# Heads turned four tiles behind their sums, attention in three pinned steps, weight sums on DVE

## The chip, the cores and the metric

The kernel runs as one program on one core of a Trainium2 chip. The core's engines work from queues of their own, each in the order in which its program stands: TensorE (PE) multiplies, VectorE (DVE), ScalarE (ACT) and GpSimd (POOL) do the elementwise work, SyncE (SP) only issues transfers. An instruction that waits for another engine holds up all that stands behind it on its own. The metric is the device time of one execution in microseconds (us), lower is better.

## The reference, cut to what matters

```python
def reference(x, mem, ...):                       # x (1, 1024, 1024) float32
    for l in range(DEPTH):                        # layer 0: attention, layer 1: HGRN2
        h = rms_norm(x, norm_gain[l])
        cols = h @ w_in                           # mixer columns | memory query | gate
        mix = dilated_mixer(...) if l % 2 == 0 else hgrn2_mixer(...)
        mem_out = memory_cross_attention(q_mem, mem, ...)
        y = concatenate([mix, mem_out]) * silu(gate)
        x = x + y @ w_out
    return x

def dilated_mixer(cols, cos, sin, q_gain, k_gain):
    qkv = cols.reshape(B, S, 3, N_GROUPS, A_HEADS, HEAD_DIM)     # 3 groups of 8 heads of 128
    q, k = rms_norm(q, q_gain), rms_norm(k, k_gain)              # over each head's 128 columns
    q, k = apply_partial_rotary(q, ...), apply_partial_rotary(k, ...)
    # causal windows (128, 1), (512, 4), (2048, 16); the groups merged by their denominators
```

## The kernel before

All products are made in float32 accuracy from halves: an operand is split into a high part (`hi`, `wh`) and a low rest (`lo`, `wl`), and three matmuls of 512 columns take the place of one. ACT makes the high part (`copy`, L154), DVE the rest (L838, L200).

The program runs in stages. First come the norm of `x`, its transposes, sums of its blocks and a chunk of the gate (to about 74 us). Then, to 853 us, come the **products**: the q, k and v columns of attention's three groups, nine blocks in the order k, v, q for groups 2, 1, 0. Each block is worked as seven products of quarter blocks in the manner of Strassen and Winograd (`product`, p = 0 to 6), each of four tiles (i = 0 to 3) of 12 matmuls, L932 to L934, into a PSUM bank `acc` of pool `pp`, which has three. The quarter weights arrive as `raw` by SP's queue; their sums and differences are made by `combine` (L842, eight for a block, on POOL), then they are split (`split_side`).

A product's tile is added to kept sums `x0` to `x3`, `y0` to `y3`. In products 1, 4, 5 and 6 this finishes 128 rows by 512 columns, four heads, of the block, held in a tile `c` (three buffers) or in `x`, `y`. For q and k a **chain** follows (`projected`, L893): DVE adds the bank (L942, L953, L957 or L960); ACT squares (L899); DVE reduces (L901) and scales (L161, `rv`); POOL takes the power (L163, `rr`); DVE multiplies (L903); POOL turns the rotary columns with four instructions (L876, L878 twice, L880); PE transposes four times (`heads_T`, L298) into a bank `pt`, of which there are two; ACT moves that into a tile `os` (L910); ACT's queue then spills it to memory, `qk_scr`: four transfers of 64 KB for groups 2 and 1 (L918), one of 256 KB for group 0 (L913). For v the sum is only spilled. So 16 chains run in each of six blocks, in bursts: four in product 1, then twelve in products 4 to 6.

The order of instructions on every engine is chosen when the program is built, by a scheduler that plans with costs of its own; the written order binds it only through data and buffers. On the chip that order is fixed.

Next is the **memory stage** (853 to 1032 us): slices of 48 matmuls of layer 0's gate for the memory output (`gate_mem`: the two of `MG0`, and the first of `MG1`, which is written at the start of attention and which the scheduler moved in here), the norm of `mem`, its products and the memory queries. Then **attention** (1032 to 1262 us): 12 pairs of heads, group 2 first, then 1, then 0, eight tiles each. `fetch` brings a pair's k, q and v (1024 KB each) into one of two buffers; per tile `scores` makes the scores (L1078), DVE's masked minimum (L1081) and ACT's exponentials (L1083), and `values` transposes them (L1093), copies that to `pts` (L1095, DVE) and multiplies by v (L1101). Every second tile of groups 2 and 1, `spill` copies the bank to one of two tiles `os` (ACT, L154) and sends it to memory (L1121, `o_scr`); in group 0 `merge` reads those again. The second slice of `MG1` stands after group 1. The rest, gate, output product and layer 1, runs to the end.

Of the kernel before, what the change touches and what calls it, by code (L numbers as in the profile page):

```python
# [30 lines left out]
D = 1024  # L31
# [71 lines left out]
def trunk_kernel(ctx, tc, x, mem, pos, norm_gain, w_in_a, q_gain_a, k_gain_a, qk_gain_t, w_out_a,  # L103
# [6 lines left out]
    const = ctx.enter_context(tc.tile_pool(name="const", bufs=1))  # L110
    hpool = ctx.enter_context(tc.tile_pool(name="hT", bufs=1))
    wpool = ctx.enter_context(tc.tile_pool(name="wring", bufs=WR))
    rpool = ctx.enter_context(tc.tile_pool(name="raw", bufs=2))
    gs = ctx.enter_context(tc.tile_pool(name="gs", bufs=2))
    small = ctx.enter_context(tc.tile_pool(name="small", bufs=6))

    small.tile([128, 40], F32, name="left", bufs=1)
    ctx.enter_context(tc.tile_pool(name="right", bufs=1, side="right")).tile([128, 56], F32, name="right")
    dram = ctx.enter_context(tc.tile_pool(name="scratch", bufs=1, space=bass.MemoryType.DRAM))
    pp = ctx.enter_context(tc.tile_pool(name="pp", bufs=3, space=PSUM))  # L120
    pS = ctx.enter_context(tc.tile_pool(name="pS", bufs=2, space=PSUM))
    pT = ctx.enter_context(tc.tile_pool(name="pT", bufs=2, space=PSUM))
    pO = ctx.enter_context(tc.tile_pool(name="pO", bufs=1, space=PSUM))
# [20 lines left out]
    V.memset(nhalf[:], -0.5)  # L144

# [24 lines left out]
    def more_weights(stack, n=2, start=0):  # L170

        more.append(stack.enter_context(tc.tile_pool(name="wmore", bufs=n, side="right")))
        more.append(WR + n)
        turn[0] = start
        stack.callback(more.clear)
# [129 lines left out]
    def mem_gains(pool):  # L305

        rows_ = pool.tile([16, 128], F32, name="mgr", bufs=1)
# [5 lines left out]
    def mem_norm(pool):  # L313

        mts = []
        for m in range(2):
            xt = pool.tile([128, D], F32, name="xt")
            Y.dma_start(xt[:], mem[m * 128:(m + 1) * 128, :])
            xn = norm_rows(xt[:], None, D, pool)
# [146 lines left out]
    def feature_proj(key):  # L466
# [3 lines left out]
        for hf in range(2):  # L470
# [7 lines left out]
            pss.append(ps)  # L478
        return pss

    def gate_slice(key, scr, pool=gs, name="os", gain=None):


        for hf, ps in enumerate(feature_proj(key)):
# [11 lines left out]
    def gate_mem(i, *where):  # L496
        gate_slice(("gate_m", i), gatem_scr[i * 128:(i + 1) * 128], *where)
# [136 lines left out]
    def begin_out_a(s2):  # L634
        assert at_piece[1] == at_piece[0] and not rooms
        more_weights(wide, W_B, WR)
        early, late = (s2.enter_context(tc.tile_pool(name=n, bufs=3, side="right")) for n in ("wearly", "wlate"))
# [3 lines left out]
        ol, oy, op = (s2.enter_context(tc.tile_pool(name=n, bufs=1)) for n in ("outl", "outy", "outp"))  # L641
# [55 lines left out]
    with ExitStack() as sa:  # L697
        atab = sa.enter_context(tc.tile_pool(name="atab", bufs=1))
# [6 lines left out]
        ext = sx.enter_context(tc.tile_pool(name="ext", bufs=1))  # L705
        sums = {(s, n): ext.tile([128, 4, 512], F32R, name=s + n) for s in ("s2", "s3", "s4") for n in ("hi", "lo")}
        wx = sx.enter_context(tc.tile_pool(name="wx", bufs=1))
# [11 lines left out]
        def tables():  # L719
# [35 lines left out]
            V.memset(gqk[0:ROT, :], 1.0)  # L755

        s0 = ExitStack()
        ipool = s0.enter_context(tc.tile_pool(name="ipool", bufs=1))
# [82 lines left out]
        def combine(gi, out, a, b, h):  # L841
            G.tensor_tensor(raws[gi, out, h], raws[gi, a, h], raws[gi, b, h], op=OP.subtract)  # L842
# [50 lines left out]
        def projected(i, g, Q, m, c):  # L893
# [14 lines left out]
            to = o[:] if g == 0 else o[:].rearrange("p h (r l) -> p h l r", r=n)  # L908
            of = t[:] if g == 0 else t[:].rearrange("p h (l r) -> p h l r", r=n)
            A.activation(to, of, AF.Copy, scale=gqk[:, g:g + 1] if i else 1.0)  # L910
            scr = qk_scr[i][g][:, 4 * Q:4 * Q + 4]
            if g == 0:
                SQ.dma_start(scr[:, :, m * 128:(m + 1) * 128], o[:])  # L913
                return
            at = m % 4 * 32 if g == 1 else m * 16
            view = scr.rearrange("p h (a r c) -> p h a r c", a=3 - g, r=n)[:, :, m // 4 if g == 1 else 0, :, at:at + RUN[g]]
            for h in range(4):
                SQ.dma_start(view[:, h], o[:, h].rearrange("p (r l) -> p r l", r=n))  # L918
# [608 lines left out]
```

## Time and profile before

| what | value |
|---|---|
| time, median of 3 runs | 2194.97 us (2194.24 to 2196.37) |
| the profiled execution | 2194.4 us, its span 2192.5 us |
| mean granted PE clock | 0.988 |
| DMA | 272.53 MB, mean 124 GB/s |
| products, 74 to 853 us | 779 us, PE busy 748.5 |
| memory stage, 853 to 1032 us | 179 us, PE busy 169.5 |
| attention, 1032 to 1262 us | 230 us, PE busy 191.2 |

A row that groups instructions names line, engine, operation and tiles; after the x its count, then the busy time, the mean in ns, and behind the bar the engine's idle time just before them and what ended it. A row of the waits reads: engine, tile and line that waited, the engine, tile and line that ended it, the sum in us, how often, the longest.

### The profile page before, as it was taken

What the parts mean: (1) busy time and instruction counts of PE and PEld (TensorE: products, weight loads), DVE (VectorE), ACT (ScalarE), POOL (GpSimd) and SP (SyncE); (2) the same over time, 40 slices, a digit from 0 to 9 for tenths busy, and PEclk for the clock granted to TensorE, in tenths of its full rate; (3) what the DMA queues carried; (4) which work ended last, traced back from release to release, by engine and by line L of the source; (5) the groups of instructions that cost most, each with busy time, mean ns of one, the idle gap of its engine ahead of it and who ended that gap; (6) DMA issues with size and microseconds to landing.
All of it is one profiled execution on the core that took longest, in us unless ns stands there. A gap on an engine that the chain in (4) does not pass through costs nothing.

```text
span 2192.5 us, 29737 instructions
## 1 busy us (share of the span) xinstructions
PE 2093.1 (95%) x10713; PEld 1744.3 (80%) x10713; DVE 1300.3 (59%) x2524; ACT 827.6 (38%) x1567; POOL 745.5 (34%) x772
## 2 busy tenths in 40 slices
PE   7999998999999999897889899999999999999999
PEld 5777876778777888686778788888888888888887
DVE  7875566745767455645556954433557772776443
ACT  5544345443444233545554322233533222232211
POOL 2777278763888366022002610011300000000221
PEclk9999999999999999999899999999999999999999
DMA  5366365452544524523886666431211112113733
GB/s 185 116 122 110 106 120 94 100 125 93 130 95 121 151 76 125 158 74 128 317 285 220 205 216 205 144 109 39 87 39 49 58 58 58 49 50 96 231 119 112
DMA packets 416322, 272.53 MB, mean 124 GB/s; under 512 B 223392, under 2 KB 347568, under 8 KB 413104
## 3 DMA queue, kind: packets, MB, share of 16 engines
q1 hardware_dynamic: 152608, 189.72, 28.2%
q10 hardware_dynamic: 263568, 80.91, 14.5%
q8 instruction: 86, 1.41, 0.3%
q14 instruction: 60, 0.49, 0.1%
HBM read 187.60 MB, written 82.97 MB: 123 GB/s over the span
## 4 chain that ended last, share of the span: by engine, by line
PE 44%; DMA 3%; DVE 2%; ACT 1%; issue 0%; ACTq 0%; POOL 0%; SPq 0%; DVEq 0%
PE acc L475 5%; PE acc L474 5%; PE acc L476 5%; PE acc L562 4%; PE acc L563 4%; PE acc L564 4%; PE acc L240 3%; PE acc L238 3%; PE acc L239 3%; DMA o_scr<-os 2%; PE pt L1282 1%; PE s L1282 1%; PE s L1078 1%; PE po L1416 1%; PE pt L281 1%; PE s L1385 1%
## 5 line engine op out<-in xcount | busy, mean ns | idle before, releaser
L163 POOL TENSOR_TENSOR rr<-rv,nhalf 128x4 f32<-128x4 f32 (+1 forms) x150 | 162.4, 1088 | 782.3 <-DVE rv L161 765.4
L154 ACT ACTIVATE wh<-raw 128x1024 fp32r<-128x1024 f32 x206 | 215.6, 1056 | 256.6 <-PE acc L934 123.6
L838 DVE TENSOR_TENSOR wl<-raw,wh 128x1024 fp32r<-128x1024 f32 x126 | 189.3, 1509 | 109.0 <-ACT wh L154 108.7
L932 PE MATMUL acc<-wh,hhi 128*128 128x512 f32 x576 | 229.4, 398 | 11.8 <-ACT x L154 11.2
L842 POOL TENSOR_TENSOR raw<-raw 128x1024 f32<-128x1024 f32 x72 | 176.5, 2470 | 170.3 <-DVE wl L838 133.9
L933 PE MATMUL acc<-wl,hhi 128*128 128x512 f32 x576 | 227.7, 395 | 0.0
L934 PE MATMUL acc<-wh,hlo 128*128 128x512 f32 x576 | 227.5, 395 | 0.0
L475 PE MATMUL acc<-hlo,wh 128*128 128x512 f32 x512 | 204.1, 399 | 0.0
L476 PE MATMUL acc<-hhi,wl 128*128 128x512 f32 x512 | 203.9, 398 | 0.0
L474 PE MATMUL acc<-hhi,wh 128*128 128x512 f32 x512 | 202.9, 396 | 0.0
L200 DVE TENSOR_TENSOR wl<-raw,wh 128x1024 fp32r<-128x1024 f32 x80 | 98.5, 1234 | 121.2 <-ACT wh L154 120.6
L240 PE MATMUL acc<-wh,hlo 128*128 128x512 f32 x384 | 151.6, 396 | 5.8 <-DVE hlo L259 5.8
L238 PE MATMUL acc<-wh,hhi 128*128 128x512 f32 x384 | 150.8, 397 | 0.8 <-ACT wh L154 0.8
L239 PE MATMUL acc<-wl,hhi 128*128 128x512 f32 x384 | 151.3, 394 | 0.0
L562 PE MATMUL acc<-wh,yhi 128*128 128x512 f32 x360 | 144.4, 403 | 0.5 <-ACT yhi L154 0.5
L563 PE MATMUL acc<-wl,yhi 128*128 128x512 f32 x360 | 142.8, 397 | 0.0
L564 PE MATMUL acc<-wh,ylo 128*128 128x512 f32 x360 | 141.5, 398 | 0.0
L932 PEld LDWEIGHTS acc<-wh,hhi 128*128 128x128 f32 x576 | 109.4, 190 | 37.2 <-ACT x L154 13.7
L934 PEld LDWEIGHTS acc<-wh,hlo 128*128 128x128 f32 x576 | 109.3, 190 | 22.4
L933 PEld LDWEIGHTS acc<-wl,hhi 128*128 128x128 f32 x576 | 109.4, 190 | 22.1 <-DVE wl L838 0.3
L474 PEld LDWEIGHTS acc<-hhi,wh 128*128 128x128 f32 x512 | 96.3, 188 | 17.9
L475 PEld LDWEIGHTS acc<-hlo,wh 128*128 128x128 f32 x512 | 96.3, 188 | 17.9
(287 smaller groups left out, 4799.1 us busy)
## 6 DMA issues: line engine op xcount, KB each, us to landing
raw<-in_w_in_a_dram SPq DMA_DIRECT2D x106, 512.0 KB, 4.2
raw<-in_w_in_b_dram SPq DMA_DIRECT2D x40, 512.0 KB, 3.7
qk_scr<-os ACTq DMA_DIRECT2D x256, 64.0 KB, 2.7
kT<-qk_scr SPq DMA_DIRECT2D x12, 1024.0 KB, 5.8
qT<-qk_scr SPq DMA_DIRECT2D x12, 1024.0 KB, 8.7
o_scr<-os ACTq DMA_DIRECT2D x96, 128.0 KB, 4.0
qk_scr<-os ACTq DMA_DIRECT2D x32, 256.0 KB, 2.2
raw<-in_w_mem_kv_dram SPq DMA_DIRECT2D x16, 512.0 KB, 3.7
```

The costliest lines, as they stand in the source:

```text
L238: T.matmul(ps, hi, wh[:, j, :], start=at == 0, stop=False)
L239: T.matmul(ps, hi, wl[:, j, :], start=False, stop=False)
L240: T.matmul(ps, lo, wh[:, j, :], start=False, stop=at == n - 1)
L474: T.matmul(ps[:], wh[:, k, :], mh, start=k == 0, stop=False)
L475: T.matmul(ps[:], wh[:, k, :], ml, start=False, stop=False)
L476: T.matmul(ps[:], wl[:, k, :], mh, start=False, stop=k == 7)
L562: T.matmul(pss[ch][:], hi[:, k, :], wh[:, j, :], start=first and k == 0, stop=False)
L563: T.matmul(pss[ch][:], hi[:, k, :], wl[:, j, :], start=False, stop=False)
L564: T.matmul(pss[ch][:], lo[:, k, :], wh[:, j, :], start=False, stop=end and k == 3)
L932: T.matmul(flat, hi, wh, start=kt == 0, stop=False)
L933: T.matmul(flat, hi, wl, start=False, stop=False)
L934: T.matmul(flat, lo, wh, start=False, stop=kt == 3)
```

## The change

- **Pools**: all take `reuse_waits="tile"`: whoever takes freed space waits for the tiles that lay there, not for their whole pool.
- **Order**: in products and attention PE's instructions are tied to the order in which they are written (`pinned`).
- **Chains**: the transposes, ACT's copy and the spill of a finished tile are a function of their own, `spill_heads`, which `passed` calls when the fourth tile in the count has passed (the third for the last tile of product 1). They are written in place into the tile that held the sum; the fourth tile of products 1 and 4 gets a room of its own (`y3`, `os`). In every second product the fourth tile goes to bank `po`. Groups 2 and 1 spill by one transfer of 256 KB.
- **Weight sums**: six of a block's eight `combine` go from POOL to DVE; those named 21' stay.
- **Memory stage**: the memory's norm is written ahead of the first gate slice, its transposes behind; the gain table is made at the start.
- **Attention**: the first pair is fetched before the memory queries into a pool of its own, and two pools take turns. A step does the scores of tile j, the transposes of tile j-1, one matmul of the gate slices (96 in 96 steps, in place of the slice that the scheduler had moved into the memory stage and the one after group 1), and the values of tile j-2. In group 0 ACT makes the copy `pts`.

```diff
-    const = ctx.enter_context(tc.tile_pool(name="const", bufs=1))
+    const = ctx.enter_context(tc.tile_pool(name="const", bufs=1, reuse_waits="tile"))
...
+    @contextmanager
+    def pinned():
+
+        traced = nc.cur_bb.bb.instructions
+        n = len(traced)
+        yield
+        mine = lambda i: i.engine == mybir.EngineType.PE
+        last = next((i for i in reversed(traced[:n]) if mine(i)), None)
+        for i in traced[n:]:
+            if mine(i):
+                if last is not None:
+                    tc.add_manual_dep(i, last.name, mybir.DependencyInfo(mybir.DependencyClass.NoSync, mybir.DependencyReason.DATA),
+                                      reason="pinned")
+                last = i
...
+    def gate_mem_steps(i):
+
+        (wh, wl), = take(("gate_m", i), 1)
+        for hf in range(2):
+            ps = pp.tile([128, 512], F32, name="acc")
+            for k in range(8):
+                mh, ml = (hT(n, k)[:, hf * 512:(hf + 1) * 512] for n in ("hi", "lo"))
+                for j, (w, m) in enumerate(((wh, mh), (wh, ml), (wl, mh))):
+                    T.matmul(ps[:], w[:, k, :], m, start=k == 0 and j == 0, stop=k == 7 and j == 2)
+                    yield
...
         def combine(gi, out, a, b, h):
-            G.tensor_tensor(raws[gi, out, h], raws[gi, a, h], raws[gi, b, h], op=OP.subtract)
+            (G if out == "21'" else V).tensor_tensor(raws[gi, out, h], raws[gi, a, h], raws[gi, b, h], op=OP.subtract)
...
-        def projected(i, g, Q, m, c):
+        tick, due = [0], []
+
+        def passed(n=1):
+
+            tick[0] += n
+            while due and due[0][0] <= tick[0]:
+                due.pop(0)[1]()
+
+        def projected(i, g, Q, m, c, after):
...
             rotary(c, m)
+            due.append((tick[0] + after, lambda: spill_heads(i, g, Q, m, c)))
+
+        def spill_heads(i, g, Q, m, c):
+
             t = heads_T(c)
-            o = gs.tile([128, 4, 128], F32, name="os")
+            o = c
...
-            view = scr.rearrange("p h (a r c) -> p h a r c", a=3 - g, r=n)[:, :, m // 4 if g == 1 else 0, :, at:at + RUN[g]]
-            for h in range(4):
-                SQ.dma_start(view[:, h], o[:, h].rearrange("p (r l) -> p r l", r=n))
+            flat = qk_scr[i][g].rearrange("p h s -> p (h s)")
+            o0, w, at = (m // 4 * 4096 + Q * 2048, 2048, m % 4 * 32) if g == 1 else (Q * 4096, 4096, m * 16)
+            SQ.dma_start(flat[:, o0:o0 + w].rearrange("p (x c) -> p x c", c=128)[:, :, at:at + RUN[g]],
+                         o.rearrange("p h (r l) -> p (h r) l", r=n))
...
-                ps = pp.tile([128, 4, 128], F32, name="acc")[:]
+                bank, name = (pO, "po") if n % 2 == 0 and i == 3 else (pp, "acc")
+                ps = bank.tile([128, 4, 128], F32, name=name)[:]
...
-                    c = room("c", bufs=3)
+                    c = room("c", bufs=3) if i < 3 else room("y3")
                     V.tensor_tensor(c, xs[i], ps, op=OP.add)
                     copy(A, xs[i], ps)
-                    projected(i_, g, 0, i, c)
+                    projected(i_, g, 0, i, c, 4 if i < 3 else 3)
...
                 weights_ahead(n, i)
+                passed()
...
-            product(n, (lambda i, h: ahead(1 + h) if i == 3 else None) if n == last else None)
+            with pinned():
+                product(n, (lambda i, h: ahead(3 + h) if i == 3 else ahead(2)) if n == last else None)
...
-                mem_gains(ipool)
-                gate_mem(MG0[0])
-                mts = mem_norm(ipool)
+                xns = mem_norm(ipool)
+                gate_mem(MG0[0], between=lambda: passed(2))
+                passed(2)
+                mts = mem_turn(ipool, xns)
                 gate_mem(MG0[1])
...
+            fetch(0)
             mem_queries("qmem_a", km, vm, *mp, lambda: mp[1].tile([128, 2, MEM], F32, name="pm")[:], om_scr, lhs_natural)
...
-                V.tensor_copy(pts[:, :2 * nb, :], t[:, :2 * nb, :])
+                copy(V if g else A, pts[:, :2 * nb, :], t[:, :2 * nb, :])
+                return g, hp, m, pts, blocks
...
-            gate_mem(MG1[0])
             fetch(1)
...
                 for m in range(NT):
-                    new = (g, hp, m, *scores(g, hp, m))
-                    if waiting:
-                        values(*waiting.pop())
-                    waiting.append(new)
-                if (g, hp) == (1, 3):
-                    gate_mem(MG1[1])
+                    with pinned():
+                        new = (g, hp, m, *scores(g, hp, m))
+                        old = turn_(*scored.pop()) if scored else None
+                        next(fill, None)
+                        if turned:
+                            values(*turned.pop())
+                    scored.append(new)
+                    if old:
+                        turned.append(old)
```

Three places in the instruction order, all in the block of k for group 1 (the fourth of nine), at the end of product 1. First PE: before, the transposes of the first tile of product 1, `c_3228`, stand here (`acc_3463` is the first tile of product 3):

```order
L933 MATMUL acc_3463<-wl_3413,s2hi_131 128x512
L934 MATMUL acc_3463<-wh_3412,s2lo_132 128x512
L298 MATMUL pt_3246<-ident_119,c_3228 128x128 x4
L298 MATMUL pt_3296<-ident_119,c_3278 128x128 x4
L932 MATMUL acc_3490<-wh_3408,s2hi_131 128x512
L933 MATMUL acc_3490<-wl_3409,s2hi_131 128x512
```

And with the change, where that tile is `c_3105` and `po_3195` is the fourth tile of product 1 itself:

```order
L983 MATMUL po_3195<-wh_3014,hhi_143 128x512
L984 MATMUL po_3195<-wl_3015,hhi_143 128x512
L985 MATMUL po_3195<-wh_3014,hlo_144 128x512
L313 MATMUL pt_3226<-ident_119,c_3105 128x128 x4
L983 MATMUL acc_3233<-wh_3123,hhi_143 128x512
L984 MATMUL acc_3233<-wl_3124,hhi_143 128x512
```

The transposes stood behind the eighth tile after the one that they turn; they now stand behind the third, the last of the burst.

On DVE, before, the first three tiles of product 1 get their multiplication (L903) in a row, and the fourth's add (`c_3364`, L942) comes later, behind two adds of product 3 (L949):

```order
L903 TENSOR_TENSOR c_3228<-c_3228,rr4_3237 128x512
L903 TENSOR_TENSOR c_3278<-c_3278,rr4_3287 128x512
L903 TENSOR_TENSOR c_3321<-c_3321,rr4_3330 128x512
L838 TENSOR_TENSOR wl_3479<-raw_2565,wh_3478 128x1024
L838 TENSOR_TENSOR wl_3483<-raw_2664,wh_3482 128x1024
L949 TENSOR_TENSOR x0_3152<-x0_3152,acc_3463 128x512
L942 TENSOR_TENSOR c_3364<-x3_3213,acc_3351 128x512
```

With the change (L881 weight sum, L993 add, L948 reduce, L176 scale, L877 low half, L950 multiply):

```order
L881 TENSOR_TENSOR raw_2582<-raw_3020,raw_2582 128x1024
L993 TENSOR_TENSOR c_3144<-x1_3044,acc_3131 128x512
L881 TENSOR_TENSOR raw_2578<-raw_2582,raw_2578 128x1024
L948 TENSOR_REDUCE ss4_3110<-s_3108 128x4
L993 TENSOR_TENSOR c_3176<-x2_3067,acc_3163 128x512
L948 TENSOR_REDUCE ss4_3149<-s_3147 128x4
L176 TENSOR_SCALAR rv4_3112<-ss4_3110 128x4
L176 TENSOR_SCALAR rv4_3151<-ss4_3149 128x4
L877 TENSOR_TENSOR wl_3249<-raw_2580,wh_3248 128x1024
L993 TENSOR_TENSOR y3_3208<-x3_3090,po_3195 128x512
L950 TENSOR_TENSOR c_3105<-c_3105,rr4_3114 128x512
L948 TENSOR_REDUCE ss4_3181<-s_3179 128x4
```

The multiplication of the first tile, `c_3105`, now stands right behind the add of the fourth, which needs `po_3195`, the last matmuls ahead of the transposes above. Two weight sums stand between the adds shown.

On POOL, before, six weight sums (L842, three of them shown) lie around the powers (L163), and the rotary of the first tile (`c_3228`) follows:

```order
L842 TENSOR_TENSOR raw_3166<-raw_2666,raw_3166 128x1024
L842 TENSOR_TENSOR raw_2664<-raw_2668,raw_2664 128x1024
L163 TENSOR_TENSOR rr4_3237<-rv4_3235,nhalf_118 128x4
L163 TENSOR_TENSOR rr4_3287<-rv4_3285,nhalf_118 128x4
L163 TENSOR_TENSOR rr4_3330<-rv4_3328,nhalf_118 128x4
L842 TENSOR_TENSOR raw_3486<-raw_2668,raw_3486 128x1024
L876 TENSOR_TENSOR t1_3240<-c_3228,rc_688 128x128
L878 TENSOR_TENSOR t2_3241<-c_3228,rs_689 128x4x16 x2
L880 TENSOR_TENSOR c_3228<-t1_3240,t2_3241 128x4x32
```

With the change (L881 weight sum, L178 power, L915 to L919 rotary):

```order
L915 TENSOR_TENSOR t1_3117<-c_3105,rc_693 128x128
L917 TENSOR_TENSOR t2_3118<-c_3105,rs_694 128x4x16 x2
L919 TENSOR_TENSOR c_3105<-t1_3117,t2_3118 128x4x32
L881 TENSOR_TENSOR raw_3347<-raw_2582,raw_3347 128x1024
L915 TENSOR_TENSOR t1_3156<-c_3144,rc_693 128x128
L917 TENSOR_TENSOR t2_3157<-c_3144,rs_694 128x4x16 x2
L178 TENSOR_TENSOR rr4_3185<-rv4_3183,nhalf_118 128x4
L178 TENSOR_TENSOR rr4_3217<-rv4_3215,nhalf_118 128x4
L919 TENSOR_TENSOR c_3144<-t1_3156,t2_3157 128x4x32
```

One weight sum of POOL is now between the rotary of the first tile and that of the second, `c_3144`, and two powers stand inside the latter. These three orders are alike in all six blocks of k and q.

More of the change, by code (lines that the diff above doesn't have):

```diff
@@ L1 @@
 import math
-from contextlib import ExitStack
+from contextlib import ExitStack, contextmanager
 import numpy as np
@@ L170, in more_weights @@
     def more_weights(stack, n=2, start=0):
-        more.append(stack.enter_context(tc.tile_pool(name="wmore", bufs=n, side="right")))
+        more.append(stack.enter_context(tc.tile_pool(name="wmore", bufs=n, side="right", reuse_waits="tile")))
         more.append(WR + n)
@@ L478, in feature_proj, with gate_slice @@
             pss.append(ps)
-        return pss
-    def gate_slice(key, scr, pool=gs, name="os", gain=None):
-        for hf, ps in enumerate(feature_proj(key)):
+            if between and hf == 0:
+                between()
+        return pss
+    def gate_slice(key, scr, pool=gs, name="os", gain=None, between=None):
+        for hf, ps in enumerate(feature_proj(key, between)):
             sg = pool.tile([128, 4, 128], F32, name=name)[:].rearrange("p h d -> p (h d)")
@@ L1085, in scores, with turn_ @@
                 return p, blocks
-            def values(g, hp, m, p, blocks):
-                q, k, v, st = held[g, hp]
+            def turn_(g, hp, m, p, blocks):
                 nb = len(blocks)
```

192 lines of the change are left out of this document (111 added, 81 removed).

## The prediction

> **What bounds the kernel now.** The page first, then PE stage by stage, then what ended its waits.
>
> ```profile
> span 2192.5 us, 29737 instructions
> PE 2093.1 (95%) x10713; PEld 1744.3 (80%) x10713; DVE 1300.3 (59%) x2524; ACT 827.6 (38%) x1567; POOL 745.5 (34%) x772
> ```
>
> PE bounds the whole, so time can be won or lost only where it idles or runs at a lower clock. In the table by stages the first number behind the comma is PE's busy time; PEclk is the granted clock.
>
> ```profile
> core 0: us, PE busy (x) PEld busy (x) DVE busy (x) ACT busy (x) POOL busy (x), PEclk, DMA share, GB/s
> 74.00:853.00 779.00, 748.50 (x3386) 605.32 (x3384) 503.29 (x644) 325.23 (x421) 535.98 (x572) 0.99 0.47 112
> 853.00:1032.00 179.00, 169.52 (x872) 140.62 (x871) 94.94 (x178) 85.17 (x177) 41.28 (x50) 0.97 0.37 111
> 1032.00:1262.00 230.00, 191.20 (x1283) 170.59 (x1283) 141.35 (x601) 113.27 (x437) 46.37 (x41) 0.94 0.78 259
> 1262.00:2192.00 930.00, 925.59 (x4923) 782.56 (x4921) 502.49 (x1003) 258.11 (x455) 95.49 (x86) 1.00 0.32 101
> ```
>
> PE idles for 30.5 us in the products, 9.5 in the memory stage, 38.8 in attention, and 4.4 in the last 930, where nothing is to be had. In the products a clock of 0.99 costs about 0.01 x 748.5 = 7.5 us more, so some 741 us are work at full clock. PE's waits, in the products and then in attention:
>
> ```profile
> PE pt L298 <- POOL c L880: 13.2, 13, 2.5
> PE acc L932 <- ACT x L154: 11.2, 6, 2.9
> ...
> PE po L1101 <- ACT os L154: 12.6, 6, 5.1
> PE s L1078 <- DMA qT<-qk_scr: 9.6, 2, 9.2
> ```
>
> In the products PE waits for the chain's last link and for banks that ACT clears late; in attention for spill tiles and, once, for the first pair.
>
> **The change in the products.** Before, the first chain's add is at 90.2 us, its transposes at 112.2:
>
> ```profile
> L942 DVE TENSOR_TENSOR c<-x,acc x36: 670/675/690, 90.2 to 807.0; 128x512 f32<-128x512 f32 x36
> L298 PE MATMUL pt<-ident,c x192: 270/272/332, 112.2 to 843.9; 128*128 128x128 f32 x192
> ```
>
> That is 22 us, and PE still waited. The order has the transposes eight tiles behind; now three. Matmuls start 0.23 us apart,
>
> ```profile
> 89.75 0.39 PE L932 MATMUL acc<-wh,hhi 128*128 128x512 f32 x1
> 89.97 0.39 PE L933 MATMUL acc<-wl,hhi 128*128 128x512 f32 x1
> ```
>
> so a tile of 12 is 2.72 us and the chain now has 8.2 us. How long is it unhindered? The lightest stretch is product 4 of the last block; its first chain, and what stands in between:
>
> ```profile
> 819.86 0.68 DVE L953 TENSOR_TENSOR c<-y,acc 128x512 f32<-128x512 f32 x1
> 820.58 0.60 ACT L899 ACTIVATE s<-c 128x512 f32<-128x512 f32 x1 [2.41 <-DVE c L953]
> 821.21 0.69 DVE L901 TENSOR_REDUCE ss<-s 128x4 f32<-128x512 f32 x1
> 821.94 0.17 DVE L161 TENSOR_SCALAR rv<-ss 128x4 f32<-128x4 f32 x1
> 822.19 1.01 POOL L163 TENSOR_TENSOR rr<-rv,nhalf 128x4 f32<-128x4 f32 x1 [0.68 <-DVE rv L161]
> 822.65 0.69 DVE L953 TENSOR_TENSOR c<-y,acc 128x512 f32<-128x512 f32 x1 [0.55 <-PE acc L934]
> 823.26 0.68 DVE L954 TENSOR_TENSOR x<-x,acc 128x512 f32<-128x512 f32 x1
> 823.86 0.68 DVE L903 TENSOR_TENSOR c<-c,rr 128x512 f32<-128x512 f32 x1
> 824.62 0.46 POOL L876 TENSOR_TENSOR t<-c,rc 128x128 f32<-128x128 f32 x1 [1.42 <-DVE c L903]
> 825.04 0.60 POOL L878 TENSOR_TENSOR t<-c,rs 128x64 f32<-128x64 f32 x2
> 826.58 0.46 POOL L880 TENSOR_TENSOR c<-t,t 128x128 f32<-128x128 f32 x1
> ```
>
> The chain takes 7.2 us (819.86 to 827.04) with the power done at 823.20; the multiplication stands until 823.86 behind the next tile's adds. **An engine's order is what counts**: DVE works 512 columns in 0.61 us, start to start, and cannot pass an add that waits for PE. With the change the first multiplication of product 1 stands behind the add of the burst's fourth tile, after whose last matmul PE has the transposes at once. From that matmul: add 0.05 + 0.61, multiply 0.69, POOL 0.08, then 0.42 + 0.57 + 0.46: PE waits **2.9 us**, whatever the load. The second chain's transposes are due 0.44 + 2.72 us later; POOL has, after the first rotary, a weight sum (2.40 from the row below), two products (0.99), two powers (0.97 each) and the last 0.46, 5.8 us in all: **2.6 us** of wait.
>
> ```profile
> L842 POOL TENSOR_TENSOR raw<-raw x72: 2352/2402/3462, 82.2 to 801.1; 128x1024 f32<-128x1024 f32 x72
> L838 DVE TENSOR_TENSOR wl<-raw,wh x126: 1207/1225/3489, 71.7 to 829.9; 128x1024 fp32r<-128x1024 f32 x126
> ```
>
> These rows also show instructions of the same size held up by about the time of one on the other engine (3462 against 2352, 3489 against 1207). DVE has a low half ready beside that weight sum, so the second wait is 2.6 to 3.8 us; I take 3.1. [...]
>
> In product 4 the multiplication stands behind two adds of the third tile: 0.05 + 2 x 0.61 + 0.17 + 0.69 + 0.08 + 1.45 = 3.7 us after it, less one tile: 1.0 us. Two later chains of that burst come 1.1 and 0.7 us late by the same count (a low half and a reduce ahead of one multiplication, powers of later tiles inside the rotary). A block: 2.9 + 3.1 + 2.8 = 8.8 us. A weight sum on DVE isn't in the trace; between 1.2 us (L838, of the same shape) and POOL's 2.4 I take 1.2: 6 x 9 x 1.2 = 65 us on an engine that is busy for 503 of 779, so free but for their place. In the three k blocks that place costs: two low halves and two sums, 4.8 us, start only when ACT is through with the spills of the block before, and the first add comes about 1.4 us late: 10.2. **Six blocks: 3 x 8.8 + 3 x 10.2 = 57 us** of waits, against 30.5 before.
>
> The clock comes on top. A wait and what followed, before:
>
> ```profile
> 620.40:623.40 3.00, 0.17 (x1) 0.00 (x0) 1.50 (x3) 1.44 (x3) 2.62 (x2) 1.00 0.56 87
> 623.40:626.90 3.50, 3.40 (x8) 2.72 (x9) 2.10 (x4) 2.00 (x5) 3.50 (x2) 0.51 0.48 75
> ```
>
> After 2.8 us without work PE had half clock for 3.4, so lost 1.7. Product 1 has two waits of such a size in each block: 6 to 12 such losses, 10 to 20 us, taken 12. [...]
>
> What is won: ACT's spills. 256 issues become 64, and ACT, which cleared banks late (11.2 us), has them clear. The price of one:
>
> ```profile
> L918 ACTq DMA_DIRECT2D qk_scr<-os x256: 366/531/2598, 114.6 to 624.6; - x128
> L913 ACTq DMA_DIRECT2D qk_scr<-os x32: 366/366/388, 643.8 to 869.6; - x32
> ```
>
> A 256 KB spill in many pieces is not in the trace: 0.37 us as in group 0, or four times 0.6; I take the first, and 2 us of bank waits left. Products: 741 + 57 + 12 + 2 = 812, that is **+33 us** (with only the waits that the order forces, 6.5 a block, and 5 of clock: +6; with 12 a block and 20 of clock: +59).
>
> **Memory stage.** 48 matmuls go out: 48 x 0.227 = 10.9 us. They covered some 3 us of waits, and the norm's squares now stand on ACT behind the gate's own work, so the 4.8 us below grow by about 2:
>
> ```profile
> PE acc L238 <- ACT mhi L154: 4.8, 1, 4.8
> ```
>
> **-6 us** (-10 to 0).
>
> **Attention.** The wait for the first qT, 9.6 us, goes, less about 2 for masks that still load late: -7.5, and some 3 of half clock with it. The slice after group 1 goes: -10.9. Its 96 matmuls are spread over 96 steps. In pairs 3 to 8 PE idles, bound by spills,
>
> ```profile
> 1061.00:1094.00 33.00, 23.94 (x160) 21.80 (x160) 13.44 (x76) 16.66 (x70) 0.00 (x0) 0.84 0.80 285
> 1094.00:1165.00 71.00, 58.14 (x405) 51.27 (x403) 35.82 (x164) 39.64 (x150) 0.00 (x0) 0.98 0.79 256
> 1181.00:1262.00 81.00, 74.34 (x496) 66.12 (x495) 74.63 (x275) 35.92 (x141) 46.37 (x41) 0.98 0.72 226
> ```
>
> for 9.1 + 12.9 = 22 us, enough to hide 48 x 0.227 = 10.9. The two spill tiles stay two, so that idling itself stays. The 16 in the first two pairs cost 3.6. In group 0 (third row) DVE is busy for 74.6 of 81 us; ACT takes over its copies,
>
> ```profile
> L1095 DVE COPY pts<-pt 128x512 f32<-128x512 f32 x44 | 30.0, 683 | 18.8 <-PE pt L1093 16.9 <-PE po L1101 1.7
> ```
>
> some 4 to 5 us a pair, so DVE no longer bounds and half of the 32 x 0.227 = 7.3 us fits into what it frees: +4. Together -7.5 - 3 - 10.9 + 3.6 + 4 = **-14 us** (-25 to 0).
>
> The pools' waits by tile touch stages with 4.4 us of idling: nothing. Sum: 2194.4 + 33 - 6 - 14 = 2207; the profiled execution is within 0.6 us of the median, so **2207 us**.
>
> **The rivals.** *The chains keep pace*: POOL is rid of six weight sums of 2.4 us a block, the chain falls to the 7.2 us above, three tiles cover it, and the 30.5 us vanish: 741 + 10 of rest in the products, -28, so 2194 - 28 - 6 - 14 = 2146, faster. It decides at 8.2 us of chain; against it stands the add of the fourth tile, which alone makes the first chain 11.1. *Waits smaller, attention freer*: only what the order forces (+6 to +15), and fewer waits for spills: 2180 to 2195. *Spills still bind*: the third step of attention saves nothing but the first wait and the slice is not hidden: 2194 + 33 - 6 - 3 = 2218. *ACT isn't relieved*: issues of 2.4 us for a spill in pieces, as much as before, banks clear late again and blocking lengthens the chain: 2225 to 2240. That the transposes aren't moved at all is excluded by the order.
>
> **Chances.** Forecast 0.51; chains keep pace 0.12; smaller waits 0.15; spills bind 0.13; ACT or blocking 0.09. The range leaves out the first rival and the worst of the last: 2178 to 2236. About 0.2% (4.4 us) is what can be told from no change: faster 0.19 (0.12, and half of the smaller waits), same 0.10, slower 0.71.
>
> **What would show it.** PE's waits for the chain's last POOL instruction should grow from 13.2 us to about 50, in pairs of some 3 us after product 1 of each k and q block, half clock behind them; the waits for banks cleared by ACT should go; the first wait of attention too. If the waits for the chain stay under 15 us, the first step is wrong, and so is the sign.

## The result and the profile after

The changed kernel takes 2257.24 us (median of 4 runs, 2256.06 to 2260.92) against 2195.33 before (median of 4): 1.0285 times as long, with an interval of 1.0267 to 1.0303. The direction was forecast, the size not: 62 us lost in place of 13, outside the range. The page of the profiled execution (2256.34 us) begins:

```profile
span 2254.5 us, 29624 instructions
PE 2110.3 (94%) x10713; PEld 1752.2 (78%) x10713; DVE 1307.1 (58%) x2546; ACT 852.4 (38%) x1599; POOL 596.4 (26%) x718
```

PE has the same number of instructions and is busy for 17 us more: some of its work ran at a lower clock (mean granted clock 0.977, before 0.988). The first and last matmul bound the stages: the products end at 928.2 us (853.5 before), the first score is at 1094.4 (1041.7 before). In the table by stages of the changed kernel, busy times in the order PE, PEld, DVE, ACT, POOL, then PEclk:

```profile
74.00:928.00 854.00, 771.39 (x3410) 621.04 (x3409) 525.14 (x701) 334.88 (x425) 394.56 (x527) 0.96 0.44 103
928.00:1094.00 166.00, 151.45 (x799) 126.57 (x798) 91.94 (x172) 82.56 (x173) 34.31 (x39) 0.97 0.41 134
```

The products take 854.4 us, 74.7 more than before. From there to the first score it is 166.2 us, 22.0 less (188.2 before); from the first score to the end 1160.1 us, 9.3 more (1150.8). 74.7 - 22.0 + 9.3 = 62.0 us. The last part falls in two: from the first score to the last value, that is attention, 247.6 us, 15.0 more (232.6), and behind it 912.5, 5.7 less (918.2). PE's waits in the products:

```profile
PE pt L313 <- DVE rv L176: 43.1, 6, 7.4
PE pt L313 <- POOL c L919: 18.4, 13, 3.1
PE pt L313 <- POOL os L919: 10.2, 6, 2.3
PE pt L313 <- POOL y L919: 4.9, 3, 1.7
PE pt L313 <- POOL x L919: 4.4, 3, 2.1
PE acc L984 <- DVE wl L877: 1.2, 1, 1.2
PE acc L983 <- ACT x L169: 0.2, 1, 0.2
```

All but 1.4 us of these 82.4 us are transposes that wait for their chain. The first row is one wait of 7.2 us in each of the six blocks of k and q: the first transposes of product 1 (the row names rv because the semaphore value that PE waits for was inferred to come with it; the rotary ended last). Where those 7 us come from is seen on DVE and POOL, here in the block of k for group 1. The columns are start, duration, engine, line, operation; in brackets stands the idle time before the instruction:

```profile
377.60 1.23 DVE L877 TENSOR_TENSOR wl<-raw,wh 128x1024 fp32r<-128x1024 f32 x1 [4.39 <-ACT wh L169]
378.86 1.23 DVE L881 TENSOR_TENSOR raw<-raw 128x1024 f32<-128x1024 f32 x1
380.00 1.22 DVE L877 TENSOR_TENSOR wl<-raw,wh 128x1024 fp32r<-128x1024 f32 x1
380.22 3.25 POOL L881 TENSOR_TENSOR raw<-raw 128x1024 f32<-128x1024 f32 x1 [6.70 <-DVE raw L881]
381.14 3.41 DVE L881 TENSOR_TENSOR raw<-raw 128x1024 f32<-128x1024 f32 x1
384.48 0.68 DVE L993 TENSOR_TENSOR c<-x,acc 128x512 f32<-128x512 f32 x1
385.07 1.21 DVE L881 TENSOR_TENSOR raw<-raw 128x1024 f32<-128x1024 f32 x1
...
389.93 1.22 DVE L877 TENSOR_TENSOR wl<-raw,wh 128x1024 fp32r<-128x1024 f32 x1
389.97 3.02 POOL L178 TENSOR_TENSOR rr<-rv,nhalf 128x4 f32<-128x4 f32 x2 [6.50 <-DVE rv L176]
...
391.06 0.68 DVE L993 TENSOR_TENSOR y<-x,po 128x512 f32<-128x512 f32 x1
392.05 0.69 DVE L950 TENSOR_TENSOR c<-c,rr 128x512 f32<-128x512 f32 x1 [0.31 <-POOL rr L178]
...
393.38 2.02 POOL L917 TENSOR_TENSOR t<-c,rs 128x64 f32<-128x64 f32 x2
395.48 0.46 POOL L919 TENSOR_TENSOR c<-t,t 128x128 f32<-128x128 f32 x1
...
395.98 1.12 PE L313 MATMUL pt<-ident,c 128*128 128x128 f32 x4 [7.44 <-DVE rv L176]
```

DVE has no gap over 0.4 us from 377.6 to 395.1. POOL's weight sum (380.22) runs into DVE's low half and takes 3.25 us, where the shortest of its 18 likes takes 2.36; DVE's next sum, beside it, takes 3.41 where its like takes 1.21. So the first add starts at 384.48, when the second tile is already done, and the fourth tile's add, which needs matmuls that ended at 388.5 (395.98 less the wait), is only at 391.06. The powers and the two products of the rotary take longer too, 3.02 us for two of 1.0 and 2.02 for what took 0.60 in the light stretch before. So of the 7.4 us 2.5 pass before the fourth tile's add, and 4.9 from it to the transposes. The clock during and after this wait:

```profile
388.60:395.90 7.30, 0.00 (x0) 0.00 (x0) 6.99 (x14) 3.53 (x6) 5.85 (x7) 0.65 0.25 72
395.90:402.00 6.10, 6.02 (x19) 4.76 (x20) 1.60 (x4) 1.41 (x2) 6.02 (x9) 0.58 0.44 102
```

For 6 us after the wait PE works at little over half clock, which costs 0.42 x 6.1 = 2.6 us. That is the worst of the six long waits: behind them PE had half clock for 2.9 to 5.1 us, 24 us together. Seven of the shorter waits (1.9 to 3.1 us) were followed by 2.9 to 3.4 us of it, 23 us together. Half of the 47 us is lost, some 23. The stage's mean clock of 0.96 would give more (0.04 x 854 = 34 us), but it counts half clock in the waits themselves too (0.65 in the first row), where PE has nothing to lose.

### The profile page after: what moved, and what is told of

It reads as the page before. It is cut to its first block, busy times and chain, and to the rows that moved or that the text cites. A ratio compares the mean times of both kernels' runs of the same rounds, so it can differ in the third digit from the quotient of the medians.

```text
span 2254.5 us, 29624 instructions
## 1 busy us (share of the span) xinstructions
PE 2110.3 (94%) x10713; PEld 1752.2 (78%) x10713; DVE 1307.1 (58%) x2546; ACT 852.4 (38%) x1599; POOL 596.4 (26%) x718
## 4 chain that ended last, share of the span: by engine, by line
PE 71%; DVE 9%; DMA 7%; POOL 5%; ACT 4%; issue 3%; ACTq 1%; SPq 0%; DVEq 0%; POOLq 0%
PE acc L983 6%; PE acc L984 6%; PE acc L985 6%; PE acc L495 5%; PE acc L496 5%; PE acc L497 5%; PE acc L600 4%; PE acc L601 4%; PE acc L602 4%; PE acc L255 4%; PE acc L254 4%; PE acc L253 4%; PE pt L313 2%; POOL rr L178 2%; PE s L1143 1%
## 5 line engine op out<-in xcount | busy, mean ns | idle before, releaser
L178 POOL TENSOR_TENSOR rr<-rv,nhalf 128x4 f32<-128x4 f32 (+1 forms) x150 | 155.8, 1041 | 842.9 <-DVE rv L176 841.8
L877 DVE TENSOR_TENSOR wl<-raw,wh 128x1024 fp32r<-128x1024 f32 x126 | 158.1, 1258 | 175.3 <-ACT wh L169 175.2
L983 PE MATMUL acc<-wh,hhi 128*128 128x512 f32 x504 | 208.6, 414 | 0.2 <-ACT x L169 0.2
L984 PE MATMUL acc<-wl,hhi 128*128 128x512 f32 x504 | 201.7, 400 | 1.2 <-DVE wl L877 1.2
L985 PE MATMUL acc<-wh,hlo 128*128 128x512 f32 x504 | 201.0, 399 | 0.0
L496 PE MATMUL acc<-hlo,wh 128*128 128x512 f32 x480 | 191.4, 399 | 0.0
L497 PE MATMUL acc<-hhi,wl 128*128 128x512 f32 x480 | 191.2, 398 | 0.0
L495 PE MATMUL acc<-hhi,wh 128*128 128x512 f32 x480 | 190.1, 396 | 0.0
L215 DVE TENSOR_TENSOR wl<-raw,wh 128x1024 fp32r<-128x1024 f32 x80 | 100.2, 1254 | 119.3 <-ACT wh L169 117.8
L255 PE MATMUL acc<-wh,hlo 128*128 128x512 f32 x384 | 151.3, 395 | 5.8 <-DVE hlo L274 5.8
L253 PE MATMUL acc<-wh,hhi 128*128 128x512 f32 x384 | 150.6, 397 | 0.8 <-ACT wh L169 0.8
L254 PE MATMUL acc<-wl,hhi 128*128 128x512 f32 x384 | 151.2, 394 | 0.0
L985 PEld LDWEIGHTS acc<-wh,hlo 128*128 128x128 f32 x504 | 97.9, 194 | 21.6
L1148 ACT ACTIVATE pa<-pa,st 128x128 f32<-128x128 f32 (+1 forms) x192 | 84.5, 441 | 69.8 <-DVE st L1146 33.2
L881 POOL TENSOR_TENSOR raw<-raw 128x1024 f32<-128x1024 f32 x18 | 50.7, 2818 | 208.5 <-DVE raw L881 172.7
```

The lines of the kernel that those rows point to most:

```text
L253: T.matmul(ps, hi, wh[:, j, :], start=at == 0, stop=False)
L254: T.matmul(ps, hi, wl[:, j, :], start=False, stop=False)
L255: T.matmul(ps, lo, wh[:, j, :], start=False, stop=at == n - 1)
L495: T.matmul(ps[:], wh[:, k, :], mh, start=k == 0, stop=False)
L496: T.matmul(ps[:], wh[:, k, :], ml, start=False, stop=False)
L497: T.matmul(ps[:], wl[:, k, :], mh, start=False, stop=k == 7)
```

## The experiments

Each is the changed kernel with the edit shown; times are compared with the kernel before by ratios of runs on the same chip. "The products" are from their first to their last matmul. They took 749.6, 751.4, 753.5 and 750.2 us in four runs with the same order of the products on PE (e2, e7, e8 and e12), so a difference of less than 4 us in them shows nothing.

**e1: the weight sums back on POOL**

```diff
-            (G if out == "21'" else V).tensor_tensor(raws[gi, out, h], ...)
+            G.tensor_tensor(raws[gi, out, h], ...)
```

> All eight weight sums of a block back on POOL, the rest as changed. Theory (three tiles are too few for the chain, and DVE's sums, which stand ahead of the adds and lock POOL, make it longer): the first wait of product 1 keeps the 2.9 us that the order forces but the chain now has POOL's sums of 2.4 us inside; the products stay at 835 to 875 us, the kernel at 2235 to 2280. Rival (the sums on DVE alone lost the time): products back at 770 to 790, kernel at 2170 to 2195.

Ratio 1.0398 (1.0368 to 1.0427), products 881.5 us, waits:

```profile
PE pt L313 <- POOL c L919: 93.2, 16, 14.6
```

A little above the theory's range for the products, inside it for the kernel (2276.09 us), and the rival falls: the sums on DVE are not what lost the time. With POOL's sums ahead of the powers a single wait grows to 14.6 us. At three tiles' distance the sums are bad in either place, worse on POOL.

**e2: eight tiles in place of four**

```diff
-                    c = room("c", bufs=3) if i < 3 else room("y3")
+                    c = room("c", bufs=3) if i < 3 else gs.tile([128, 4, 128], F32, name="os")[:]
...
-                    projected(i_, g, 0, i, c, 4 if i < 3 else 3)
+                    projected(i_, g, 0, i, c, 8)
...
-                    projected(i_, g, 0, 4 + i, xs[i], 4)
+                    projected(i_, g, 0, 4 + i, xs[i], 8)
```

(and 8 in products 4 and 6 too; the memory stage lets 12 pass.)

> The transposes eight in the count behind (seven whole tiles between) in place of four, the fourth tile of product 1 in a tile os; nothing else. Theory: waits of PE for the chain fall from 82 us to under 15, half clock with them, products to 750 to 775 us, kernel to 2150 to 2180. Rival (the pinned order as such, or the sums on DVE, cost the time, whatever the distance): products stay above 820, kernel above 2220.

Ratio 0.9843 (0.9819 to 0.9868), 2155.15 us: the distance, with the room that the fourth tile needs for it, turns 2.8% of loss into 1.6% of gain. In the products (749.6 us) no wait for a chain's POOL end is left among the waits, and the clock is full:

```profile
73.00:822.00 749.00, 737.57 (x3374) 600.65 (x3373) 522.11 (x696) 326.79 (x419) 410.84 (x516) 1.00 0.49 116
```

The order is as pinned as in the changed kernel and the sums stand on DVE as there; the rival falls.

**e3: the products' order left to the scheduler**

```diff
-            with pinned():
+            if True:
                 product(n, ...)
```

> The products' PE order left to the scheduler again (attention stays pinned); it then puts four to eight whole tiles between a tile and its transposes. Theory (distance counts): products 755 to 790 us, kernel 2160 to 2195. Rival (the pinned order is not at fault): within 15 us of the changed kernel, 2240 to 2270.

Ratio 0.9878 (0.9849 to 0.9907), products 765.1 us, kernel 2163.93; both times lie in the theory's ranges. Without the pin the scheduler itself moves the transposes back, to four to seven whole tiles behind theirs. That is 15 us short of e2; its waits for chains are short but many:

```profile
PE pt L313 <- POOL c L919: 8.4, 7, 2.0
PE pt L313 <- POOL y L919: 7.8, 8, 1.3
```

So the pin as such cost nothing that shows (e2 is pinned); a pin at too short a distance does.

**e5 and e6: the sums taken out**

Both kernels leave out work that the result needs, so they serve for the time alone.

```diff
e5:
-            (G if out == "21'" else V).tensor_tensor(raws[gi, out, h], raws[gi, a, h], raws[gi, b, h], op=OP.subtract)
+            return
e6:
-            (G if out == "21'" else V).tensor_tensor(raws[gi, out, h], raws[gi, a, h], raws[gi, b, h], op=OP.subtract)
+            if out != "21'":
+                V.tensor_tensor(raws[gi, out, h], raws[gi, a, h], raws[gi, b, h], op=OP.subtract)
```

> As changed (transposes three whole tiles behind), with all weight sums of the products left out, on DVE and POOL; the split takes the loaded weights instead. Theory (the order alone forces 2.9 us a block, all above that comes from the sums in DVE's queue and from the lock): PE's first wait of product 1 falls from 7.4 to 2.9 to 3.5 us, the second from 3.1 to under 1.5, all waits for chains in the products from 81 to 25 to 45 us, the products from 854 to 785 to 815 us. Rival (the chain is as long without sums): products above 835.

> As changed, with only the 18 weight sums that stay on POOL (named 21') left out. Theory: the DVE sum that stood locked for 3.4 us takes 1.2, so the first wait of product 1 falls from 7.4 to about 5 us; the second, which had POOL's sum inside the chain, from 3.1 to under 1.5; products 815 to 840 us. Rival (no lock, only DVE's load): first wait above 6.8, products above 840.

Timed once each: 2208.11 us with no sums, 2237.84 with POOL's 18 left out; products 808.1 and 836.0 us, both inside the theories' ranges. The transposes of the first two tiles of product 1, in the block of q for group 1 (the sixth), first without POOL's 18 sums, then as changed:

```profile
564.64 1.12 PE L313 MATMUL pt<-ident,c 128*128 128x128 f32 x4 [5.18 <-POOL c L920]
```

```profile
577.52 1.12 PE L313 MATMUL pt<-ident,c 128*128 128x128 f32 x4 [7.34 <-DVE rv L176]
583.19 0.66 PE L313 MATMUL pt<-ident,c 128*128 128x128 f32 x4 [0.21 <-POOL c L919]
```

e6 keeps the order of adds, reduces and multiplications, and its theory's number for the first wait holds: 2.2 us of it (7.34 - 5.18) are POOL's 18 sums. The DVE sum that took 3.42 us in this block takes 1.22 without them (lines are one higher in that kernel):

```profile
551.94 1.22 DVE L882 TENSOR_TENSOR raw<-raw 128x1024 f32<-128x1024 f32 x1
```

Of the 5.18 us that are left, 2.9 are what the prediction counted for the order; the fourth add is 0.9 late (560.37, for matmuls that ended at 559.46), and the first rotary takes 2.85 us in place of 1.45.

e5 does not measure the order's price, since without the sums the scheduler chose another order on DVE. There the first tile's multiplication stands ahead of the third and the fourth tile's add, in all six blocks, and the first transposes don't wait at all. The 2.80 us stand before those of the second tile:

```profile
539.39 0.69 DVE L950 TENSOR_TENSOR c<-c,rr 128x512 f32<-128x512 f32 x1 [1.12 <-POOL rr L178]
...
542.75 0.60 PE L313 MATMUL pt<-ident,c 128*128 128x128 f32 x4
543.10 0.68 DVE L993 TENSOR_TENSOR y<-x,po 128x512 f32<-128x512 f32 x1
...
548.89 1.12 PE L313 MATMUL pt<-ident,c 128*128 128x128 f32 x4 [2.80 <-POOL c L919]
```

So its theory's "2.9 to 3.5" for the first wait is not what happened, and that the order alone forces 2.9 us is worked out from rows of before and shown by no run. All waits for chains come to 48.0 us in e5, just over its range of 25 to 45.

Both theories also speak of a second wait of 3.1 us in product 1. As changed there is none of that size: the second transposes waited at most 0.95 us. The 3.1 us belong to the first chain of product 4, which waits 2.5 to 3.1 us in five of the six blocks, here in k for group 1:

```profile
436.44 0.66 PE L313 MATMUL pt<-ident,c 128*128 128x128 f32 x4 [2.62 <-POOL c L919]
```

In e6 this wait stays (2.5 to 3.2 us). In e5 it is gone, and the third chain of product 4 waits 1.5 us instead.

**e4: more spill tiles in attention**

```diff
-                os = ap_.tile([128, 4, 128], F32, name="os")
+                os = ap_.tile([128, 4, 128], F32, name="osp", bufs=4)
```

> Attention's spill of groups 2 and 1 gets four tiles of its own in place of two, the rest as changed. Theory (ACT stands behind a spill tile's transfer and the exponentials behind ACT, so that PE waits for pa): attention of groups 2 and 1 from 139 us to 115 to 128, kernel 2232 to 2248. Rival (the chain of scores, exponentials and transposes itself is too long for one step, or transfers bind): attention within 4 us, kernel 2253 to 2260.

Ratio 1.0294 (1.0264 to 1.0324), 2254.81 us: nothing, and the theory falls; the time is where the rival had it. PE's waits in attention of the changed kernel, and with four tiles:

```profile
PE pt L1157 <- ACT pa L1148: 25.1, 24, 4.4
```

```profile
PE pt L1157 <- ACT pa L1148: 25.7, 25, 3.6
```

Before, PE waited here for spill tiles (12.6 us) and for pa 6.2. Now it is pa alone: PE comes to a tile's transposes one step after its scores. The worst issue of a spill in the changed kernel:

```profile
1101.21 0.29 DVE L1146 CUSTOM_DVE_ANT_0 pa<-s,masks 128x128 f32<-128x128 f32 x1
...
1101.74 1.34 ACTq L1190 DMA_DIRECT2D o_scr<-os  x1
1101.75 0.61 PE L1143 MATMUL s<-kT,qT 128*128 128x128 f32 x4
...
1103.13 0.40 ACT L1148 ACTIVATE pa<-pa,st 128x128 f32<-128x128 f32 x1 [1.31 <-DVE st L1146]
...
1103.67 0.33 PE L1157 MATMUL pt<-ident,pa 128*128 128x128 f32 x1 [1.20 <-ACT pa L1148]
```

The minimum of this tile's second head (1101.21) was done 1.6 us before its exponential (1103.13). Issuing a spill held ACT's queue for 1.34 us in between, and PE waits 1.2 us. The median of the 64 issues is 0.34 us, but they come in pairs, and in most of the 24 waits one stands right ahead of the exponential; in the longest, 4.4 us, ACT's idle time is put down to a transfer. More spill tiles changed nothing of the sum. How much of the 25.1 us is the issues was not varied.

**e7 and e8: attention with the distance of e2 in the products**

```diff
e7:
-                    with pinned():
+                    if True:
                         new = (g, hp, m, *scores(g, hp, m))
e8:
-                p = ap_.tile([128, 2, 256], F32, name="pa", bufs=3)
+                p = ap_.tile([128, 2, 256], F32, name="pa", bufs=4)
...
-                        old = turn_(*scored.pop()) if scored else None
+                        old = turn_(*scored.pop(0)) if len(scored) > 1 else None
```

> As e2 (eight tiles in the count), and attention's PE order left to the scheduler; its steps and fillers stay. Theory (the pinned order binds PE to the chain of scores, exponentials, transposes one step long): first score to last value from 252 to 225 to 242 us, kernel 2128 to 2147. Rival (the 96 matmuls and the transfers set attention's time, not the order): 247 to 256, kernel 2150 to 2160.

> As e2, attention pinned, but a tile's transposes stand two steps behind its scores in place of one (one more tile pa), the values one step behind them as before. Theory (one step is shorter than DVE's minimum and ACT's exponentials, with ACT held by spills): PE's waits for pa fall from 27 us to under 10, first score to last value from 252 to 228 to 242 us, kernel 2130 to 2147. Rival (transfers set the pace): waits move to other tiles, 247 to 256, kernel 2150 to 2160.

Ratios 0.9731 (0.9708 to 0.9754) and 0.9721 (0.9693 to 0.9750). From the first score to the last value it is 251.7 us in e2, 230.9 in e7, 226.7 in e8, as the theories have it or a little less. The two times can't be told apart. The waits for pa go from 27.9 us to 1.4 and 3.8; in e8:

```profile
PE pt L1157 <- ACT pa L1148: 3.8, 5, 1.3
```

Again not the pin but the distance: one step is too short for scores, minimum, exponentials. The 25 us of e8 over e2 lie in groups 2 and 1 (118.1 us against 143.3); group 0 stays between 108 and 109 in all three.

**e9 to e12: what the other parts are worth, from e8**

```diff
e9: all sums on POOL, as e1
e10:
-            SQ.dma_start(flat[:, o0:o0 + w].rearrange("p (x c) -> p x c", c=128)[:, :, at:at + RUN[g]],
-                         o.rearrange("p h (r l) -> p (h r) l", r=n))
+            to = flat[:, o0:o0 + w].rearrange("p (x c) -> p x c", c=128)
+            for h in range(4):
+                SQ.dma_start(to[:, h * n:(h + 1) * n, at:at + RUN[g]], o[:, h].rearrange("p (r l) -> p r l", r=n))
e11: 6 in place of 8 in products 1, 4, 5 and 6
e12: all reuse_waits="tile" taken out
```

> As e8 (eight tiles, two steps), with all weight sums back on POOL. Theory (seven whole tiles, 19 us, cover a chain of about 17 us with sums on DVE, but not the 22 us that it had with them on POOL): PE waits for chains again, products from 753 to 765 to 785 us, ratio to before 0.978 to 0.988. Rival (at this distance it doesn't matter where the sums are): products 750 to 757, ratio 0.970 to 0.975.

> As e8, with four transfers of 64 KB in place of one of 256 KB for each spill of groups 2 and 1. Theory (256 issues of 0.5 to 0.6 us keep ACT from clearing banks): waits of acc for ACT return, 4 to 12 us in the products, ratio 0.975 to 0.979. Rival (ACT has time to spare once the chain isn't waited for): products within 3 us, ratio 0.971 to 0.974.

> As e8, with six in the count (five whole tiles, 13.6 us) in place of eight. Theory (a chain of product 1 takes some 17 us with the sums on DVE, those of products 4 to 6 about 11): one wait of 2 to 4 us in product 1 of each block, products 765 to 785, ratio 0.978 to 0.988. Rival (what the scheduler's own four to eight tiles show: less is enough): products 750 to 757.

> As e8, with every pool's reuse_waits by tile taken out again. Theory (no stage waits for a whole pool): within 4 us of e8, ratio 0.970 to 0.974, the part after attention 912 to 914 us. Rival (it is what the 918 to 912 us behind attention came from): that part back at 917 to 919, ratio 0.974 to 0.977.

| | ratio to before | products, us |
|---|---|---|
| e8 | 0.9721 (0.9693 to 0.9750) | 753.5 |
| e9, sums on POOL | 0.9817 (0.9796 to 0.9838) | 767.4 |
| e10, four spills | 0.9872 (0.9849 to 0.9895) | 776.2 |
| e11, six tiles | 0.9829 (0.9808 to 0.9850) | 768.2 |
| e12, pools as before | 0.9768 (0.9747 to 0.9789) | 750.2 |

Waits of e9 and e11, one row each:

```profile
PE pt L313 <- POOL c L919: 15.0, 6, 4.0
```

```profile
PE pt L313 <- POOL c L919: 21.5, 12, 4.0
```

e8 ran on another chip than e9 to e12, each beside the kernel before; so ratios are compared, and the products' times. e9 and e11 came into the theories' ranges: with the sums on POOL even seven tiles are 1.3 to 4.0 us short for one chain of each block, and with the sums on DVE five tiles are short for one to three. At seven tiles the place of the sums is worth 14 us of products. e10 cost more than either side expected, 23 us of products: issues of 0.52 to 0.54 us (median, 366 ns the shortest) come back 256 times on ACT. PE's waits for banks that ACT clears are 10.8 us there (5.8 in e8), as the theory had it; all waits together are 26.7 against 13.4, and PE is busy for 9 us more at a clock of 0.99.

In e12 the theory holds as far as times go: 2139.62 us is 3.4 above e8, and the part behind attention is at 913.9 us (912.5 in e8) and not at 917 to 919. The ratio lies where the rival had it, but its interval touches e8's, and its profiled execution is 1.2 us shorter than e8's. An effect of the pools' waits is not shown, nor is one of 0.3% excluded. What shortened the part behind attention from 918.2 to 912.5 us stays open.

The best versions are e8, 2136.20 us, and e7, 2137.35: 2.8 and 2.7% faster than before. e8 is 5.4% faster than the changed kernel, and it is the change with two distances corrected. The new order of the memory stage, the early fetch and ACT's copies in group 0 were not varied by any run.

## Why the prediction missed

The direction held, and so did the place where it said that the time would be lost: transposes that their order puts too close behind the chain. Of the terms the first wait and the clock were too small, the other waits came at other places than forecast, and attention had the wrong sign.

- *"PE waits 2.9 us, whatever the load"* is the step that failed: 43.1 / 6 = 7.2 us. The count started at the fourth tile's last matmul and took DVE to be free there, and POOL undisturbed. The rows above show neither. The fourth tile's add came 2.5 us after those matmuls and not 0.05: the sums that the change adds stand in front of the adds in the same order that the prediction read, and one of them was held for 3.41 us. From the add to the transposes it was 4.9 us and not 2.8, since the powers and the rotary's products took longer beside DVE's work (3.02 and 2.02 us in the rows). The prediction weighed this blocking for the second wait only. 6 x 4.3 = 26 us. e6 shows 2.2 of the 4.3 us to be POOL's 18 sums; the rest is read from the rows and not varied by itself.
- *The other waits*: 57 - 6 x 2.9 = 39.6 us forecast, 82.4 - 43.1 = 39.3 measured. This agreement is luck. The second chains of product 1 were to wait 6 x 3.1 = 18.6 us and waited 2.5: their chains went on while PE stood in the long first wait. The chains of products 4 to 6 were to wait 6 x 2.8 = 16.8 and waited 35. The late first adds of the k blocks, 4.2, don't show: first waits are 7.1 to 7.4 us in k blocks and 7.1 to 7.3 in q blocks. What lengthens the waits behind products 4 to 6 was not taken apart. The pairs of some 3 us that were to show it did not come.
- *The clock, "6 to 12 such losses, taken 12"*: 13 losses of 1.8 us, 23 us. Their size was right, their number was not. In e5, where no wait for a chain is over 2.9 us, the clock still took some 11 us by an estimate: PE was busy there for 758.8 us with 3412 matmuls, against 771.4 with 3410 in the changed kernel, so 12.6 of the 23 us less. So the first waits were not all that this term hung on. The 5 us of clock in the sum for the forced waits alone (+6) are shown by no run; the clock cost 23 us in the changed kernel, some 11 in e5, and in e2, where no wait for a chain's POOL end is left, it was granted in full (1.00).
- Together: waits 82.4 for 59 (57 and 2 for banks) and clock 23 for 12 make 34 of the 42 us by which the products missed (812 forecast, 854 measured). Another 4 are 19 matmuls of the gate's chunk (19 x 0.227) that ran ahead of the products' first matmul and now run behind it. The last 4 stay open.
- *ACT's banks and the price of one spill*: 0.37 us was the right choice, the median of the 256 KB spills in pieces is 366 to 374 ns. PE's waits for ACT's banks went from 11.2 to 0.2 us, but in that kernel PE waits for chains instead: in e8, where it doesn't, 5.8 us are back. e10 shows what the larger transfers are worth where the distance is right: 23 us.
- *The memory stage and the first wait*: forecast -6 and -7.5, together -13.5 to the first score; -22.0 measured. The first wait for qT went, as forecast.
- *Attention behind the first score*: forecast -3 (half clock behind the first wait) -10.9 + 3.6 + 4 = -6.3; +9.3 measured to the end of the kernel, of which attention itself is +15.0. The wait for spill tiles went, where the prediction kept it and meant to hide 48 matmuls in it, and a larger one came that it did not have: pa, 25.1 us after 6.2. e8 shows it to be the one step between scores and transposes. The prediction read the chain in the products against its distance in tiles, and did not do the same in attention. The part behind attention, forecast at nothing, gave 5.7 us back.
- Of the rivals, "the chains keep pace" is refuted by the 82 us. "ACT isn't relieved" was nearest in time, 2225 to 2240; its condition, issues of 2.4 us, did not come (0.37 us), the blocking that it names beside it did (3.41 us for a sum of 1.21). "Spills still bind" came nearer for attention, with the wrong wait.

## What to carry to other kernels

Where an order is pinned, take for each consumer the distance to its producer in time, and set it against the whole latency of the chain between, with everything that the same change puts in front of it on each engine; not against the unhindered chain. A distance that is too short cost twice here: 82 us of waits brought a loss of 23 us at half clock with them. And where a change looks wrong as a whole, vary its one number before taking it back: the same edits at seven tiles and two steps were worth 2.8%.

## What the runs showed of the hardware

POOL's instructions took longer beside DVE's, also tiny ones: two powers on 128x4 took 3.02 us beside a DVE weight half (389.97 in the rows of the changed kernel), against 1.0 each in the light stretch before. That is read from rows and was not varied by itself. The other way round was varied: a DVE sum that took 3.42 us beside a sum on POOL took 1.22 in e6, where that one is left out.

Half clock came after some waits of 1.9 to 3.1 us and not after others. In e5:

```profile
546.20:548.90 2.70, 0.01 (x1) 0.01 (x1) 1.84 (x3) 0.63 (x2) 2.63 (x4) 0.86 0.88 222
548.90:553.00 4.10, 4.10 (x12) 3.42 (x13) 1.51 (x3) 1.07 (x1) 2.78 (x6) 0.50 0.74 203
642.00:644.70 2.70, 0.02 (x1) 0.03 (x1) 1.85 (x3) 0.57 (x1) 2.62 (x4) 1.00 1.00 265
644.70:648.10 3.40, 3.40 (x18) 2.85 (x19) 1.31 (x3) 0.69 (x1) 2.42 (x5) 1.00 0.68 227
```

2.7 us without work, then 4.1 at 0.50; and in the next block 2.7 us without work, then full clock. In the changed kernel a wait of 1.94 us up to 448.6 was followed by 3.4 us at 0.53, and one of 2.62 us up to 436.4 by 3 us at full clock (1.00). So the length of the wait alone does not settle it; what does was not shown.
